# The lo parts of 22 projection weights made by ScalarE and an accumulating transfer

## The chip, the cores and the metric

The kernel runs on one core of one Trainium2 chip. The metric is device time in microseconds (us) of one execution, taken as the median of three runs. The profile is one execution of the same program, recorded by the hardware profiler.

## The reference

One layer of a diffusion backbone: 128 context tokens and 1024 latent tokens, width 1024, in float32. After a modulated RMS norm, one projection gives queries, keys and values of four heads, two halves of a convolution channel, and 16 blocks of gates. Then come differential attention, a depthwise convolution of width 31, their gated merge, an output projection, and a gated MLP. Cut to what matters here:

```python
proj = h @ lp['w_in']                       # q, k, v, u (convolution), g (gates)
a = softmax(s1) - lam * softmax(s2)         # s1, s2: scores of the two halves of q and k
attn_out = rmsnorm(a @ v).reshape(B, T, ATTN_W) @ lp['w_attn_proj']
glu = u[..., :CONV_CH] * sigmoid(u[..., CONV_CH:])
cv = silu(layernorm(dwconv(glu, lp['w_conv_dw'])))       # DW_WIDTH = 31
merged = sigmoid(g[..., :D_MODEL]) * attn_out + sigmoid(g[..., D_MODEL:]) * (cv @ lp['w_conv_proj'])
```

## The kernel before

All large products are made of fp32r matmuls on split operands: x = hi + lo, where hi is x rounded to fp32r and lo the rest. `mm3` (L242) does three matmuls for each block of 128 x 128 weights: hi·hi, hi·lo and lo·hi. A weight unit is a tile of 128 x 1024 (512 KB). SyncE loads it into a `raw` tile (two buffers, L144); ScalarE copies it to `whi` (L180); then `wlo` = raw - whi is made, by a subtraction on GpSimd (L187), or, for most units of the up projection (`by_dma`), by a ScalarE pass that writes minus hi (L183) and a transfer issued on GpSimd that adds raw to it (L184). `whi` and `wlo` have three buffers each. `prep_to` does this for all units up to a position of the sequence SEQ; `take` hands a unit out and notes how far to prepare next: in a projection unit, once its first third is drained, the next two units are prepared.

The attention (`phase1`) runs as four heads of nine query tiles. Each tile has two score products (S, L786 and L787, one tile of three banks), VectorE's minimum (mx, L793), ScalarE's exponential (e, L795), VectorE's weighted difference of the two (e, L806), transposes on TensorE (T, L819) with their split into hi (ath, L822, ScalarE) and lo (atl, L823, VectorE), and the product with the values (O, L834). Between these steps a generator, `fillers`, feeds the matmuls of 22 projection units named in FILL (q1 to q3, k1 to k3, ua2, ub2, ua3, ub3 and gates g0 to g11), paced by a table of numbers. The units q and k go through rope products on GpSimd (L558 to L567). Each `ub` unit starts a depthwise convolution of 31 taps: for each tap VectorE multiplies and adds 967 columns (conv, L651), ScalarE multiplies the other 200 (tap, L658, one buffer) and GpSimd adds them (L664). The split is the constant CSPLIT = 967. The gate units after g11 are named TAIL and are prepared like all others.

Which instruction comes next on an engine is laid out when the program is built: the tile framework simulates a timeline (`schedule_with_timeline_sim=True`) and lists instructions by priority and by the simulated times; attention steps carry a higher priority (HP), and `pin` ties the orders of SyncE, TensorE and VectorE to the written one within a window. On the chip each engine runs its list in order, so a waiting instruction holds up all that follow it on its engine. On GpSimd these are the rope products, the tap sums, the lo subtractions and its transfers.

Of the kernel before, what the change touches and what calls it, by code (L numbers as in the profile page):

```python
# [83 lines left out]
def _w_order():  # L84
    order = ["q0", "k0", "ua0", "ub0", "ua1", "ub1", "v0", "v1", "v2", "v3"]
    fill = FILL_SEQ.split()
    tail = [f"g{i}" for i in range(16) if f"g{i}" not in fill]
    merge = [f"m{j}" for j in range(8)]
    wo = [f"wo{j}" for j in range(8)]
    up = [f"{c}{i}" for i in range(NFF) for c in ("fa", "fb")]  # L90
    down = [f"d0_{h}" for h in range(2)] + [f"e{g}_{u}" for g in range(1, NGRP) for u in range(4)]

    ffn = up[:2] + [f"w{i}_{u}" for i in range(1, NFF) for u in range(4)] + down
    return order, fill, tail, merge, wo, up, down, ffn


ORDER, FILL, TAIL, MERGE, WO, UP, DOWN, FFN = _w_order()
# [12 lines left out]
class Kernel:  # L110
# [80 lines left out]

    def by_dma(self, name):

        if name[0] != "w" or name[1] == "o":
            return False
        i, u = map(int, name[1:].split("_"))
        return i > 1 and u < 3
# [1722 lines left out]
```

## Time and profile before

| | us |
|---|---|
| median of three runs | 1790.59 |
| lowest, highest | 1790.53, 1791.32 |
| the profiled execution | 1790.29 |
| its span, first to last instruction | 1788.3 |
| mean granted TensorE clock | 0.982 |

In the views, PE is TensorE, PEld its weight loads, DVE VectorE, ACT ScalarE, POOL GpSimd and SP SyncE; L187 is line 187 of the kernel. A stretch such as 345:420 is in us from the first instruction. The V products of the attention run up to about 190 us, the heads with their fillers from there to about 705, the merge from there to some 860, then the output projection, the up projection (about 1000 to 1490) and the down projection.

### The profile page before, as it was taken

What the parts mean: (1) busy time and instruction counts of PE and PEld (TensorE: products, weight loads), DVE (VectorE), ACT (ScalarE), POOL (GpSimd) and SP (SyncE); (2) the same over time, 40 slices, a digit from 0 to 9 for tenths busy, and PEclk for the clock granted to TensorE, in tenths of its full rate; (3) what the DMA queues carried; (4) which work ended last, traced back from release to release, by engine and by line L of the source; (5) the groups of instructions that cost most, each with busy time, mean ns of one, the idle gap of its engine ahead of it and who ended that gap; (6) DMA issues with size and microseconds to landing.
All of it is one profiled execution on the core that took longest, in us unless ns stands there. A gap on an engine that the chain in (4) does not pass through costs nothing.

```text
span 1788.3 us, 25510 instructions
## 1 busy us (share of the span) xinstructions
PE 1682.3 (94%) x9928; PEld 1644.2 (92%) x9928; DVE 1177.2 (66%) x1594; ACT 751.1 (42%) x1166; POOL 713.3 (40%) x507
## 2 busy tenths in 40 slices
PE   5999989989989999889989899999999999999997
PEld 3889989978989999888989899999999999999997
DVE  5859995699697663587588765766567565333335
ACT  4424444445454554311225744545455456111111
POOL 2545782585673431544243321222222137433311
PEclk8999999999999999999999999999999999999999
DMA  8264323323325433666753364756666567622102
GB/s 312 88 190 137 103 79 104 132 69 118 120 76 182 142 105 114 235 221 205 268 174 106 85 173 114 182 131 162 150 151 150 139 148 224 175 89 101 62 12 106
DMA packets 111087, 251.96 MB, mean 141 GB/s; under 512 B 10964, under 2 KB 61816, under 8 KB 108920
## 3 DMA queue, kind: packets, MB, share of 16 engines
q1 hardware_dynamic: 45264, 120.15, 19.7%
q10 hardware_dynamic: 51592, 79.08, 13.9%
q0 software_dynamic: 14112, 51.12, 13.4%
q8 instruction: 78, 1.28, 0.3%
q14 instruction: 41, 0.34, 0.1%
HBM read 161.55 MB, written 57.30 MB: 122 GB/s over the span
## 4 chain that ended last, share of the span: by engine, by line
PE 52%; DVE 18%; DMA 8%; issue 8%; POOL 5%; ACT 3%; ACTq 1%; POOLq 0%; DVEq 0%; SPq 0%
PE f L242 15%; PE T L242 7%; DVE conv L651 7%; PE S L1499 6%; PE f L1499 6%; PE T L1499 6%; PE O L242 3%; PE O L1499 3%; DVE mx L793 2%; DMA tg<-scr_gscr 2%; PE O L834 2%; DVE e L806 2%; POOL wlo L187 1%; DVE S L1206 1%; DMA hx<-in_ada 1%
## 5 line engine op out<-in xcount | busy, mean ns | idle before, releaser
L187 POOL TENSOR_TENSOR wlo<-raw,whi 128x1024 fp32r<-128x1024 f32 x104 | 270.2, 2599 | 389.0 <-ACT whi L180 370.8
L242 PE MATMUL f<-h1h,whi 128*128 128x384 f32 x680 | 233.4, 345 | 3.9 <-ACT gt L614 3.2
L242 PE MATMUL f<-h1l,whi 128*128 128x384 f32 x680 | 234.5, 345 | 0.0
L180 ACT CAST whi<-raw 128x1024 fp32r<-128x1024 f32 x126 | 132.0, 1048 | 243.7 <-DMA raw<-in_wst 59.4
L242 PE MATMUL f<-h1h,wlo 128*128 128x384 f32 x680 | 232.0, 342 | 0.0
L1491 DVE SCALAR_TENSOR_TENSOR X<-X,vec,X 128x1153 f32<-128x1153 f32 x88 | 139.7, 1593 | 91.6 <-ACT X L1489 91.0
L651 DVE SCALAR_TENSOR_TENSOR conv<-glu,vec,conv 128x967 f32<-128x967 f32 x120 | 199.2, 1660 | 1.1
L664 POOL TENSOR_TENSOR conv<-conv,tap 128x200 f32<-128x200 f32 x120 | 115.5, 962 | 68.3 <-ACT tap L658 65.8
L242 PEld LDWEIGHTS f<-h1h,whi 128*128 128x128 f32 x680 | 130.2, 192 | 5.3 <-ACT gt L614 3.9
L242 PEld LDWEIGHTS f<-h1l,whi 128*128 128x128 f32 x680 | 130.7, 192 | 0.4
L242 PEld LDWEIGHTS f<-h1h,wlo 128*128 128x128 f32 x680 | 130.2, 192 | 0.2
L795 ACT ACTIVATE e<-S,mx 128x1152 f32<-128x1152 f32 (+1 forms) x72 | 81.2, 1128 | 70.2 <-DVE mx L793 58.7
L793 DVE TENSOR_REDUCE mx<-S 128x1 f32<-128x1152 f32 (+1 forms) x72 | 88.6, 1231 | 31.5 <-PE S L787 31.5
L658 ACT ACTIVATE tap<-glu,vec 128x200 f32<-128x200 f32 x120 | 55.5, 462 | 105.6 <-POOL conv L664 89.9
L242 PE MATMUL T<-ff,whi 128*128 128x384 f32 x360 | 92.1, 335 | 1.5 <-ACT hx L1691 1.5
L184 POOL DMA_DIRECT2D wlo<-rawx x40 | 34.4, 860 | 141.6 <-ACT wlo L183 122.9
L242 PE MATMUL f<-ff,whi 128*128 128x384 f32 x340 | 87.0, 335 | 0.5 <-ACT hx L1691 0.5
L786 PE MATMUL S<-K,q 128*128 128x384 f32 (+1 forms) x200 | 69.0, 345 | 13.3 <-ACT e L795 13.3
L823 DVE TENSOR_TENSOR atl<-T,ath 128x512 fp32r<-128x512 f32 (+1 forms) x100 | 52.0, 538 | 30.3 <-ACT ath L822 29.8
L1251 DVE SCALAR_TENSOR_TENSOR hx<-f,g,hx 128x128 f32<-128x128 f32 (+1 forms) x64 | 31.6, 515 | 58.8 <-PE f L242 58.8
L180 ACT CAST whi<-rawx 128x1024 fp32r<-128x1024 f32 x42 | 44.0, 1047 | 62.0 <-PE S L1499 23.7
L1251 DVE SCALAR_TENSOR_TENSOR hx<-T,g,hx 128x256 f32<-128x256 f32 (+1 forms) x66 | 32.3, 511 | 54.7 <-PE T L242 54.3
(438 smaller groups left out, 4961.6 us busy)
## 6 DMA issues: line engine op xcount, KB each, us to landing
raw<-in_wst SPq DMA_DIRECT2D x105, 512.0 KB, 4.2
wlo<-rawx POOLq DMA_DIRECT2D x40, 512.0 KB, 6.0
X<-scr_fscr POOLq DMA_DIRECT2D x20, 576.0 KB, 5.0
scr_fscr<-X SPq DMA_DIRECT2D x22, 512.0 KB, 5.3
wlo<-raw POOLq DMA_DIRECT2D x20, 512.0 KB, 4.8
scr_gscr<-gate ACTq DMA_DIRECT2D x48, 192.0 KB, 2.0
tg<-scr_gscr SPq DMA_DIRECT2D x24, 384.0 KB, 4.2
ada<-in_ada SPq DMA_DIRECT2D x8, 1024.0 KB, 9.9
```

The costliest lines, as they stand in the source:

```text
L180: nc.scalar.copy(hi, raw)
L187: eng.tensor_tensor(out=lo, in0=raw, in1=hi.bitcast(F32), op=ALU.subtract)
L242: nc.tensor.matmul(out, lhsT=a, rhs=b, start=(i == 0), stop=(i == n - 1))
L651: t = nc.vector.scalar_tensor_tensor(out=o, in0=glu[:, j:j + CSPLIT], scalar=w[:, j:j + 1], in1=o, op0=ALU.mult, op1=ALU.add)
L658: nc.scalar.activation(out=p, in_=glu[:, CSPLIT + j:CONVW + j], func=AF.Copy, scale=w[:, j:j + 1])
L664: t = nc.gpsimd.tensor_tensor(out=o, in0=o, in1=p, op=ALU.add)
L786: nc.tensor.matmul(S[:, j, :cw], lhsT=qt[:, c, o:o + 128], rhs=self.K[:, c, ks], start=True, stop=False)
L793: nc.vector.tensor_reduce(out=mx[:, 1:2], in_=src, axis=AX.XY, op=ALU.min)
L795: nc.scalar.activation(out=e[:, :w].rearrange("p (a b) -> p a b", a=nk), in_=src, func=AF.Exp, scale=-1.0, bias=mx[:, 1:2], accum_out=self ...
L1251: nc.vector.scalar_tensor_tensor(out=d, in0=ps[:, o:o + ln], scalar=gate[:, j, c:c + 1], in1=d, op0=ALU.mult, op1=ALU.add)
L1491: nc.vector.scalar_tensor_tensor(out=y[:, :L], in0=u[:, t:t + L], scalar=w[:, t:t + 1], in1=y[:, :L], op0=ALU.mult, op1=ALU.add)
L1499: nc.tensor.matmul(ps[:, :CH], lhsT=a[:, ws], rhs=b[:, k], start=first and k == 0 and i == 0, stop=last and k == 3 and i == 2)
```

## The change

`by_dma` returns true for every unit in FILL as well. For these 22 units the lo part is then made by a ScalarE pass (L183 in the kernel before) and an accumulating transfer (L184) in place of GpSimd's subtraction (L187). CSPLIT and everything else written in the kernel stay.

```diff
     def by_dma(self, name):
 
+        if name in FILL:
+            return True
         if name[0] != "w" or name[1] == "o":
             return False
         i, u = map(int, name[1:].split("_"))
```

## Rows read from the trace of the kernel before

**Rows 1.** The page, part 1: busy us, share of the span, instructions.

```profile
PE 1682.3 (94%) x9928; PEld 1644.2 (92%) x9928; DVE 1177.2 (66%) x1594; ACT 751.1 (42%) x1166; POOL 713.3 (40%) x507
```

**Rows 2.** Stretches: length, busy PE, PEld, DVE, ACT, POOL; clock, DMA share, GB/s.

```profile
186.00:212.00 26.00, 23.40 (x140) 23.09 (x139) 25.79 (x23) 11.83 (x24) 19.18 (x15) 0.93 0.27 83
212.00:260.00 48.00, 42.41 (x248) 40.24 (x247) 45.90 (x42) 24.58 (x48) 39.00 (x25) 0.96 0.29 79
...
345.00:420.00 75.00, 66.31 (x392) 61.95 (x391) 72.48 (x69) 38.79 (x77) 61.18 (x38) 0.98 0.34 92
...
460.00:560.00 100.00, 90.72 (x546) 86.95 (x545) 90.98 (x91) 49.80 (x100) 71.73 (x47) 0.98 0.32 94
560.00:705.00 145.00, 143.79 (x926) 142.12 (x925) 85.05 (x131) 76.50 (x148) 46.24 (x44) 1.00 0.37 127
```

**Rows 3.** The chain's shares by line, in 186:212, 345:420 and 460:560.

```profile
by line: DVE conv L651 78.5%; issue 11.4%; DVE e L806 6.2%; DVE mx L793 4.9%; DVE e L1018 3.9%; DVE mx L804 0.4%; DVE mx L803 0.3%
...
by line: DVE conv L651 39.1%; DVE e L806 16.3%; DVE mx L793 13.5%; DVE atl L823 7.2%; PE f L242 6.5%; ACT e L795 3.4%; PE T L819 2.9%; DVE mx L804 1.9%; issue 1.9%; DVE sw L550 1.8%; DVE conv L648 1.4%; ACTq L775 0.8%; DVE mx L803 0.8%; PE 
...
by line: DVE conv L651 39.5%; DVE mx L793 14.0%; DVE e L806 9.6%; PE f L242 8.2%; DVE atl L823 7.6%; issue 3.6%; PE O L834 3.1%; POOL conv L664 2.1%; POOL ors L917 1.8%; DVE conv L648 1.7%; DVE sw L550 1.5%; DVE mx L804 1.4%; PE S L786 1.1%
```

**Rows 4.** Groups by line, GpSimd, 160:605: count, busy us, mean ns, idle before.

```profile
L187 POOL TENSOR_TENSOR wlo<-raw,whi 128x1024 fp32r<-128x1024 f32 x23 | 63.0, 2739 | 90.7 <-ACT whi L180 73.5 <-issue 17.0
```

**Rows 5.** The line of the convolution's taps: ns min/median/max, first and last start.

```profile
L651 DVE SCALAR_TENSOR_TENSOR conv<-glu,vec,conv x120: 1208/1385/3457, 123.1 to 564.6; 128x967 f32<-128x967 f32 x120
```

**Rows 6.** Timelines of VectorE and GpSimd, 192:203 and 356:361: start, us, instruction.

```profile
194.48 3.03 DVE L651 SCALAR_TENSOR_TENSOR conv<-glu,vec,conv 128x967 f32<-128x967 f32 x1
...
193.30 3.19 POOL L187 TENSOR_TENSOR wlo<-raw,whi 128x1024 fp32r<-128x1024 f32 x1
...
197.88 3.36 POOL L187 TENSOR_TENSOR wlo<-raw,whi 128x1024 fp32r<-128x1024 f32 x1
...
359.26 2.08 DVE L651 SCALAR_TENSOR_TENSOR conv<-glu,vec,conv 128x967 f32<-128x967 f32 x1
...
357.02 3.30 POOL L187 TENSOR_TENSOR wlo<-raw,whi 128x1024 fp32r<-128x1024 f32 x1
```

**Rows 7.** The chain in order of time, in 140:262: start, us, what.

```profile
199.02 3.25 DVE conv L651
...
235.37 3.29 POOL wlo L187
```

**Rows 8.** The subtraction L187 alone by stretches: length, busy DVE, POOL.

```profile
186.00:212.00 26.00, 0.00 (x0) 6.55 (x2) 0.93 0.27 83
...
345.00:420.00 75.00, 0.00 (x0) 9.04 (x3) 0.98 0.34 92
460.00:560.00 100.00, 0.00 (x0) 10.73 (x4) 0.98 0.32 94
```

**Rows 9.** Lines L183 and L184: ns min/median/max, starts; the transfers' landing.

```profile
L183 ACT ACTIVATE wlo<-whi x60: 1040/1061/1073, 1015.5 to 1466.4; 128x1024 fp32r<-128x1024 f32 x60
...
L184 POOL DMA_DIRECT2D wlo<-rawx x40: 850/859/874, 1023.5 to 1467.7; - x40
...
DMA to landing us min/median/max: 4.5/5.6/10.1
```

**Rows 10.** TensorE's waits in 186:605: us in total, times, longest.

```profile
PE S L786 <- ACT e L795: 13.0, 12, 2.6
```

**Rows 11.** Waits of all engines in 205:705: us in total, times, longest.

```profile
POOL wlo L187 <- ACT whi L180: 97.1, 17, 18.1
...
ACT tap L658 <- POOL conv L664: 57.3, 41, 7.1
```

**Rows 12.** ScalarE's timeline: the hi part of g0, the last drain of q1.

```profile
192.19 1.03 ACT L180 CAST whi<-raw 128x1024 fp32r<-128x1024 f32 x1
...
213.66 0.47 ACT L606 ACTIVATE xs<-f 128x384 f32<-128x384 f32 x1
```

**Rows 13.** DMA queues in 1000:1470: packets, MB, share of 16 engines.

```profile
q0 software_dynamic: 8716, 31.77, 36.5%
```

## The prediction, made before the change was built

> **What bounds the kernel now.** I read the page's busy shares first: TensorE is busy 94% of the span, GpSimd 40%, ScalarE 42% [rows 1]. What GpSimd does matters only where TensorE waits, so I went on by stretches, around the 22 filler units, whose lo parts are made between 168 and 604 us. In the table of stretches [rows 2] read TensorE's and VectorE's busy time against the length. In 186:212, 345:420 and 460:560 VectorE is busy 25.79 + 72.48 + 90.98 = 189 of 201 us, GpSimd 152, and TensorE sits idle 2.6 + 8.7 + 9.3 = 20.6 us; in 212:260 it is idle 5.6 us. In 560:705 it is idle 1.2 of 145 us. So the attention has stretches bound by VectorE (where the convolution's taps run) and stretches bound by TensorE, and an edit here can win at most some 26 us, plus what the granted clock (0.93 to 0.98 there, 1.00 in 560:705) gives back. The chain's shares by line say the same [rows 3]: VectorE's lines make 94% of the chain in 186:212, 82% in 345:420 and 75% in 460:560 (conv, e, mx, atl, sw added up).
>
> **What the change removes.** `by_dma` becomes true for the 22 names in FILL, nothing else. So 22 of the 104 subtractions on GpSimd go. In 160:605 the 23 of them (22 of fillers and v3) take 63.0 us, 2.74 us each [rows 4]. What that is worth on VectorE is read from convolution taps that ran beside one. A tap takes 1.21 us at the least, 1.385 at the median [rows 5]. The one that began at 194.48 beside the subtraction of 193.30 took 3.03; the one at 359.26 beside that of 357.02 took 2.08 [rows 6]; the one at 199.02, beside the subtraction that began at 197.88 and took 3.36, took 3.25 [rows 6, 7]. Against the median these are 1.65, 0.70 and 1.87 us, mean 1.4. The subtractions stretch too, from 2.36 at the least to above 3.
>
> The Trainium skill, "SBUF — State Buffer", section "Who interferes with whom", says that a VectorE instruction with two SBUF inputs contends with a GpSimd instruction that reads SBUF, and that the second to issue is blocked until the first ends. By it a tap could lose a whole subtraction, and the term below would be nearly twice as large; the rows agree that they contend but show both sides losing a part, so the rows' price is used.
>
> The three stretches hold 2 + 3 + 4 = 9 subtractions [rows 8]. 9 x 1.4 = 12.6 us of VectorE time; weighted by the chain's share (94% for 2, 82% for 3, 75% for 4, mean 82%) 10.3 us at most reach the chain. Of that I take half, **5.2 us gained**: GpSimd is 76% busy in these stretches, so its next rope product or tap sum moves into most of the freed time and meets VectorE there; and where VectorE gets ahead, the next thing late is a score bank or a ScalarE copy. Ends: 0 and 10.3.
>
> In 212:260 a subtraction stands on the chain itself, 3.29 us at 235.37 [rows 7], between two rope products. An issue of 0.86 us there would save 2.4. **1.5 gained**, since what follows is waiting for ScalarE soon after; ends 0 and 2.4.
>
> **What it adds.** Each unit gets a second ScalarE pass, minus hi, of 1.06 us [rows 9]: 22 x 1.06 = 23.3 us, 12 of them (12.7 us) in the four stretches where TensorE waits (the 9, and 3 in 212:260). ScalarE is half busy there, for example 38.79 of 75 us [rows 2]. A copy costs time where an exponential stands behind it: TensorE waited for the exponential 13.0 us, 12 times, in 186:605 [rows 10], about 3% of that stretch, and its own row makes 3.4% of the chain in 345:420 [rows 3]. I take a tenth of the 12.7, **1.3 lost**; ends 0 and 12.7.
>
> The accumulating transfer's issue holds GpSimd 0.86 us in place of 2.74. It waits for the lo pass, so GpSimd stands about 1.06 us longer at that place when it comes early; behind it are the convolution's tap sums and the rope products, and ScalarE's taps wait for the tap sums (57.3 us, 41 times, up to 7.1) [rows 11]. Wait and issue together, 1.9 us, are less than the subtraction, so nothing is charged; the end on the bad side is 1.06 us for each of the 9, if every such wait is on the chain, and the good side is a gain of 0.8 each. GpSimd waits for hi already, 97.1 us in 205:705 [rows 11], mostly where it has nothing else.
>
> The lo part lands later: 1.06 + 0.86 + 5.6 us (10.1 at the most) [rows 9] after hi, 7.5 to 12.0 us, instead of 2.4 to 3.4. Cover: the unit g0, one of the two with the least slack, has hi ready at 193.2, and the unit ahead of it drains its last bank at 213.66 [rows 12], 20.4 us later. Later fillers are prepared two units ahead. Nothing is charged. The raw tile is freed some 5 us later, and so SyncE's next raw load starts later; that queue carries only raw loads here, and the same slack covers it. The transfers themselves: 60 of them, with the other accumulating traffic small, took 36.5% of 16 engines over 470 us [rows 13], 2.9 us each; the DMA share of 0.32 to 0.34 in the long stretches [rows 2] would rise to about 0.45. Nothing charged, ends 0 and 2 us.
>
> The Trainium skill, the same page, section "SBUF: two separate sides", speaks against the change: a transfer issued on GpSimd has its descriptors written there, and VectorE instructions in a two-port mode keep it from that. By it some landings would be later still, at VectorE's pleasure. The issue rows agree with no such delay at the issue (850 to 874 ns over 40); where the landing suffers is the third rival below.
>
> The planner lays out every engine's order anew from changed costs, so the places of score, tap and filler work shift by more than the edit. No row prices that; the nearest are a stretch of 48 us in which TensorE idles 5.6 us (212:260) and one of 145 us in which it idles 1.2 (560:705) [rows 2]. About their difference, 4 us, goes to either side in the range, and nothing in the sum. Sum: 5.2 + 1.5 - 1.3 = 5.4 us. The profiled execution took 1790.29 us (its span 1788.3, with 2.0 around it), so 1784.9; the median of the runs is 0.3 above it: **1785 us**.
>
> **The rivals.**
> 1. *The freed time doesn't reach TensorE.* VectorE waits instead for the scores and the exponential, and GpSimd's next work takes the place of the subtraction. For it: GpSimd's 76% in the same stretches, and ScalarE's waits for tap sums. Gains of 0 to 3 us: 1790, from 1787 to 1794. 0.23.
> 2. *Slower: the lo passes get ahead of the exponentials* in the loop score, minimum, exponential, next score, in 212:260, 345:420 and 460:560, where the bank of scores is single. Price 1.06 us a copy; it decides from the seventh of the 12, as 7 x 1.06 eats the 6.7 gained. With all 12: 12.7 - 6.7 = 6 us lost, 1796; without the gain, 1803. For it: 13.0 us of waiting for the exponential; against: ScalarE is half idle there, and its lines make under 5% of the chain in 345:420. 0.17.
> 3. *Late lo parts*: TensorE waits for a landing. It needs one more than 20 us after hi where 12.0 is the most the rows give; each would cost the excess, some us. 1793. 0.02.
> 4. *More than forecast*: the stretches are bound by VectorE and GpSimd together, and the whole 10.3 + 2.4 comes, with 1 to 3 us of the clock that the idle time costs: 1776 to 1780, here 1777. For it: 189 of 201 us busy. 0.12.
> 5. The edit does nothing, because no name matches: FILL is the split list of unit names that `prep_to` passes. 1790. 0.01.
>
> **How the numbers follow.** The forecast, 1781 to 1787, has 0.45. A difference under 0.2% (3.6 us) is about what a measurement of this kernel can't tell from none. Faster by more: 0.45 + 0.12 = 0.57. Within: 0.23 + 0.01 = 0.24. Slower: 0.17 + 0.02 = 0.19. The range goes from rival 4's end to the middle of rival 2's, 1776 to 1797, and leaves out some 0.15.
>
> **What would show it.** Right: GpSimd's subtractions 82, accumulating issues 82, ScalarE's minus-hi passes 82; GpSimd busy some 42 us less over the span, ScalarE 23 more; the mean tap nearer 1.4 than it is, and no 3 us taps beside a weight's preparation; TensorE's idle time between 186 and 605 down by about 5 us, and the merge beginning as much earlier. Wrong: taps shorter but TensorE's idle time unchanged (rival 1); more waiting of score matmuls for the exponential (rival 2); filler matmuls waiting for a transfer (rival 3). I would also be wrong if the gain of the attention were given back in the merge or later, by an order that the planner changed there.

## The result and the profile after

The changed kernel took 1805.65 us in the median (1802.37 to 1810.62, six runs) beside 1791.13 for the kernel before (1790.53 to 1794.21, six runs): ratio 1.0085, interval 1.0073 to 1.0097. It is 15 us slower where 5 us faster had been forecast, and above the end of the range. Single executions of some kernels here went far slower, at a lower granted clock (one of e5 below: 2053.62 us at 0.751), and the ratios leave those out. Lines behind `by_dma` have moved by two: the taps are L653 (L650 the first tap), the rope products L560 and L564, tap sums L666, gates L619, transposes T L821, the split atl L825, the value product O L836.

The edit did what it says. First row: busy us, share and count of each engine, against [rows 1]; then the groups of the three lines that make lo parts (count, busy us, mean ns, idle before).

```profile
PE 1686.6 (94%) x9928; PEld 1648.2 (91%) x9928; DVE 1168.0 (65%) x1594; ACT 771.0 (43%) x1188; POOL 649.3 (36%) x507
...
L187 POOL TENSOR_TENSOR wlo<-raw,whi 128x1024 fp32r<-128x1024 f32 x82 | 209.3, 2554 | 301.0 <-ACT whi L180 297.3
L184 POOL DMA_DIRECT2D wlo<-raw x42 | 36.9, 879 | 219.0 <-ACT wlo L183 125.3
L183 ACT ACTIVATE wlo<-whi 128x1024 fp32r<-128x1024 f32 x82 | 86.6, 1059 | 2.9 <-DMA qz<-scr_qscr 1.5
L184 POOL DMA_DIRECT2D wlo<-rawx x40 | 34.0, 851 | 142.1 <-ACT wlo L183 123.3
```

GpSimd is busy 64 us less, VectorE 9 us less, ScalarE 20 us more, and yet the span grew from 1788.3 to 1803.5. The same stretches as [rows 2]:

```profile
186.00:212.00 26.00, 23.53 (x137) 23.21 (x136) 25.75 (x26) 14.87 (x29) 14.88 (x18) 0.93 0.55 139
212.00:260.00 48.00, 42.47 (x250) 40.82 (x249) 43.47 (x44) 27.65 (x53) 35.10 (x26) 0.96 0.43 108
345.00:420.00 75.00, 63.44 (x361) 60.51 (x361) 70.28 (x65) 35.81 (x70) 43.65 (x33) 0.91 0.39 100
460.00:560.00 100.00, 86.75 (x511) 83.95 (x510) 84.80 (x82) 51.53 (x101) 56.01 (x48) 0.93 0.41 110
560.00:705.00 145.00, 139.78 (x876) 136.69 (x875) 88.67 (x124) 77.47 (x142) 38.49 (x44) 0.99 0.47 145
```

TensorE does less in 345:420 (63.44 for 66.31 us), in 460:560 (86.75 for 90.72) and in 560:705 (139.78 for 143.79), at a lower granted clock. To place the loss I numbered the matmuls (9928 in both traces) and took the start of each after the change minus its start before: -2.2 us at 250, +2.5 at 300, +1.0 at 340, **+9.5 at 355**, 6.5 at 520, **+14.6 at 535**, 13.0 at 595, **+18.4 at 610**, 15.2 at the end. So at 250 us the kernel is 2.2 us ahead, and then it loses at a few places, two of which, at 355 and 535, look alike. The second of these, as a timeline of GpSimd, VectorE and the waiting matmul (start, us, engine, line, instruction, idle before):

```profile
523.86 0.87 POOL L184 DMA_DIRECT2D wlo<-raw  x1 [0.98 <-PE O L836]
524.27 12.47 DVE L653 SCALAR_TENSOR_TENSOR conv<-glu,vec,conv 128x967 f32<-128x967 f32 x1
...
524.47 2.21 POOL L560 TENSOR_TENSOR sw<-sw,cst 128x1024 f32<-128x1024 f32 x1
...
526.35 2.19 POOL L560 TENSOR_TENSOR xs<-xs,cst 128x1024 f32<-128x1024 f32 x1
...
528.21 0.82 POOL L666 TENSOR_TENSOR conv<-conv,tap 128x200 f32<-128x200 f32 x1
...
530.66 2.27 POOL L560 TENSOR_TENSOR xs<-xs,cst 128x1024 f32<-128x1024 f32 x1
532.62 0.80 POOL L666 TENSOR_TENSOR conv<-conv,tap 128x200 f32<-128x200 f32 x1
533.11 2.59 POOL L564 TENSOR_TENSOR xs<-xs,sw 128x1024 f32<-128x1024 f32 x1
...
537.39 0.58 PE L836 MATMUL O<-atl,V 128*128 128x256 f32 x1 [7.92 <-DVE atl L825]
```

One tap took 12.47 us; none in the kernel before took more than 3.46 [rows 5]. It began while GpSimd issued an accumulating transfer and ended 1.04 us after the last of seven GpSimd instructions that follow the issue without a wait. VectorE's queue stood behind it, and TensorE 7.92 us behind that; the granted clock then fell to the lower of its two levels for 13.7 us (stretch: length, busy PE, PEld, DVE, ACT, POOL; clock, DMA share, GB/s):

```profile
533.20:546.90 13.70, 8.94 (x34) 8.25 (x35) 12.21 (x12) 3.06 (x7) 3.05 (x3) 0.50 0.04 13
```

At 346 us the first tap (L650, 715 ns at the least) took 6.86 us, to the end of such a stretch and 0.53 us more; in that stretch, though, a weighted difference had got its turn before (342.66 to 345.09). Look at the starts and lengths of GpSimd's instructions: 526.35 comes 0.33 us before 524.47 + 2.21. Each record overlaps the next by about 0.3 us, where it is 0.03 to 0.06 us between back-to-back instructions of the kernel before. I call GpSimd instructions that follow a transfer's issue without a wait a run.

Not every run keeps VectorE out. At 389.80 the same seven instructions follow an issue without a wait, and here VectorE gets its turn: the tap of 390.97 ends 1.02 us after the first product, and none behind it takes more than 2.86 us.

```profile
389.65 1.39 DVE L808 SCALAR_TENSOR_TENSOR e<-e,mx 128x1152 f32<-128x1152 f32 x1
...
389.80 0.87 POOL L184 DMA_DIRECT2D wlo<-raw  x1 [0.63 <-ACT wlo L183]
...
390.41 2.40 POOL L560 TENSOR_TENSOR sw<-sw,cst 128x1024 f32<-128x1024 f32 x1
...
390.97 2.86 DVE L653 SCALAR_TENSOR_TENSOR conv<-glu,vec,conv 128x967 f32<-128x967 f32 x1
```

TensorE's waits in 186:620 (us in total, times, longest) name the places:

```profile
PE T L821 <- DVE atl L825: 12.6, 8, 5.5
...
PE O L836 <- DVE atl L825: 8.9, 2, 7.9
PE f L244 <- ACT gate L619: 4.3, 2, 3.0
```

The third step, at 600 to 610, is of another kind: a filler waits 3.0 us for a gate's copy out of PSUM, ScalarE for the write-out of the columns before.

### The profile page after: what moved, and what is told of

Read it like the earlier page. It is cut to its first block, busy times and chain, and to the rows that moved or that the text cites. A ratio compares the mean times of both kernels' runs of the same rounds, so it can differ in the third digit from the quotient of the medians.

```text
span 1803.5 us, 25581 instructions
## 1 busy us (share of the span) xinstructions
PE 1686.6 (94%) x9928; PEld 1648.2 (91%) x9928; DVE 1168.0 (65%) x1594; ACT 771.0 (43%) x1188; POOL 649.3 (36%) x507
## 5 line engine op out<-in xcount | busy, mean ns | idle before, releaser
L187 POOL TENSOR_TENSOR wlo<-raw,whi 128x1024 fp32r<-128x1024 f32 x82 | 209.3, 2554 | 301.0 <-ACT whi L180 297.3
L653 DVE SCALAR_TENSOR_TENSOR conv<-glu,vec,conv 128x967 f32<-128x967 f32 x120 | 193.9, 1616 | 1.2
L666 POOL TENSOR_TENSOR conv<-conv,tap 128x200 f32<-128x200 f32 x120 | 102.5, 855 | 110.8 <-ACT tap L660 107.7
L244 PEld LDWEIGHTS f<-h1h,whi 128*128 128x128 f32 x680 | 131.3, 193 | 11.5 <-ACT gate L619 4.9
L184 POOL DMA_DIRECT2D wlo<-raw x42 | 36.9, 879 | 219.0 <-ACT wlo L183 125.3
L183 ACT ACTIVATE wlo<-whi 128x1024 fp32r<-128x1024 f32 x82 | 86.6, 1059 | 2.9 <-DMA qz<-scr_qscr 1.5
L184 POOL DMA_DIRECT2D wlo<-rawx x40 | 34.0, 851 | 142.1 <-ACT wlo L183 123.3
L825 DVE TENSOR_TENSOR atl<-T,ath 128x512 fp32r<-128x512 f32 (+1 forms) x100 | 52.2, 540 | 36.0 <-ACT ath L824 35.6
```

Source lines behind the costliest of these rows:

```text
L183: nc.scalar.activation(out=lo, in_=hi.bitcast(F32), func=AF.Copy, scale=-1.0)
L184: nc.gpsimd.dma_start(out=lo.bitcast(F32), in_=raw, accum_op=ALU.add)
L187: eng.tensor_tensor(out=lo, in0=raw, in1=hi.bitcast(F32), op=ALU.subtract)
L244: nc.tensor.matmul(out, lhsT=a, rhs=b, start=(i == 0), stop=(i == n - 1))
L653: t = nc.vector.scalar_tensor_tensor(out=o, in0=glu[:, j:j + CSPLIT], scalar=w[:, j:j + 1], in1=o, op0=ALU.mult, op1=ALU.add)
L666: t = nc.gpsimd.tensor_tensor(out=o, in0=o, in1=p, op=ALU.add)
```

## The experiments

Each experiment's time is the median of its runs, taken beside runs of the kernel before on the same chip; "ratio" is against those, with its interval. e6, e15, e16 and e18 leave out the right lo parts of the 22 units (hi, minus hi or raw stands in their place) and keep the number of matmuls.

| run | us | ratio | interval | longest VectorE instruction, 200:560 |
|---|---|---|---|---|
| kernel before | 1789.6 to 1792.3 | 1 | | 3.51 |
| changed kernel | 1805.65 | 1.0085 | 1.0073 to 1.0097 | 12.47 |
| e1_sixteen | 1794.12 | 1.0026 | 1.0015 to 1.0036 | 3.49 |
| e2_six | 1815.13 | 1.0141 | 1.0125 to 1.0156 | 12.79 |
| e3_tiny | 1807.03 | 1.0097 | 1.0077 to 1.0117 | 8.04 |
| e4_act | 1799.58 | 1.0047 | 1.0030 to 1.0064 | 3.49 |
| e5_traffic | 1796.28 | 1.0036 | 1.0022 to 1.0051 | 3.52 |
| e6_relief | 1787.91 | 0.9991 | 0.9981 to 1.0001 | 3.63 |
| e15_no_transfer | 1787.33 | 0.9982 | 0.9969 to 0.9994 | 3.25 |
| e16_no_pass | 1779.54 | 0.9941 | 0.9923 to 0.9959 | 3.77 |
| e18_plain | 1796.10 | 1.0030 | 1.0020 to 1.0041 | 4.96 |
| e8_late | 1803.96 | 1.0071 | 1.0058 to 1.0085 | 3.77 |
| e12_break | 1800.10 | 1.0054 | 1.0036 to 1.0071 | 9.98 |
| e17_break2 | 1799.88 | 1.0054 | 1.0041 to 1.0067 | 7.94 |
| e13_break_gate | 1818.41 | 1.0153 | 1.0130 to 1.0177 | 10.46 |
| e20_neg_first | 1807.40 | 1.0098 | 1.0085 to 1.0111 | 8.90 |
| e21_neg_break | 1806.61 | 1.0092 | 1.0079 to 1.0105 | 10.80 |
| e22_five | 1797.41 | 1.0040 | 1.0028 to 1.0051 | 4.21 |
| e23_twelve | 1790.07 | 0.9999 | 0.9990 to 1.0009 | 3.49 |

My theory after the first look: a transfer issued by GpSimd directly ahead of back-to-back work makes that work one run which keeps VectorE out to its end. Rivals: back-to-back work alone does it; the transfer's traffic does it; the loss is in ScalarE's passes; or in the order that the planner laid out anew.

### What keeps VectorE out: a small kernel of its own

It computes nothing of the layer; its outputs are zero. A VectorE multiply-add of 967 columns starts beside 0, 3, 6 or 9 GpSimd multiplications, with or without a transfer issued ahead:

```python
def c_big():  trigger(), dma_big(), run(6), dve_two(), close()   # accumulating, 512 KB
def c_tiny(): trigger(), dma_tiny(), run(6), dve_two(), close()  # plain, 4 KB
def c_gap():  trigger(), dma_big(), run(3), dve_two(); ...wait for ScalarE...; run(3, g3), close()
```

> A small kernel of its own; nothing of the reference is computed, all outputs are zero. Nine cases, three times each: a VectorE instruction over 967 columns starts about 1 us into a run of GpSimd multiplications of 128x1024 with no waits between them. Theory (an issue on GpSimd just ahead of a run makes its instructions follow each other without a gap, and VectorE's is kept out to the end of the run): alone 1.1 to 1.2 us; 6 multiplications without a transfer ahead, 2 to 3.5 us; with an accumulating transfer of 512 KB ahead, 4 to 5 us for a run of 3, 10 to 12 for 6, 16 to 18 for 9; with a transfer of 4 KB ahead of 6, again 10 to 12; with a wait put into the middle of the 6, 4 to 5; the same with a one-input VectorE instruction. Rival A (back-to-back work on GpSimd is enough): 6 without a transfer takes as long as 6 with one. Rival B (the traffic does it): 512 KB long, 4 KB as short as without.

Timelines: six multiplications without a transfer, with the accumulating one, with the small one.

```profile
25.58 5.56 POOL L40 TENSOR_TENSOR P<-P,g 128x1024 f32<-128x1024 f32 x2 [25.13 <-ACT g L29]
26.48 2.46 DVE L43 SCALAR_TENSOR_TENSOR D<-g,w,E 128x967 f32<-128x967 f32 x1 [3.43 <-ACT g L30]
...
109.82 0.88 POOL L33 DMA_DIRECT2D acc<-g  x1 [3.94 <-ACT g L29]
110.42 14.09 POOL L40 TENSOR_TENSOR P<-P,g 128x1024 f32<-128x1024 f32 x6
110.50 15.04 DVE L43 SCALAR_TENSOR_TENSOR D<-g,w,E 128x967 f32<-128x967 f32 x1 [3.60 <-ACT g L30]
...
242.31 0.59 POOL L36 DMA_DIRECT2D tiny<-g  x1 [3.94 <-ACT g L29]
242.92 13.81 POOL L40 TENSOR_TENSOR P<-P,g 128x1024 f32<-128x1024 f32 x6
242.99 14.77 DVE L43 SCALAR_TENSOR_TENSOR D<-g,w,E 128x967 f32<-128x967 f32 x1 [3.59 <-ACT g L30]
```

Alone the multiply-add takes 1.10 to 1.23 us. Beside six multiplications without a transfer it waits for the first one's end (27.92), takes its 1.02 us and is done at 28.94; the second multiplication waits for it in turn (3.26 us for 2.34). With a transfer ahead it took 8.2 behind 3 multiplications, 15.04 behind 6, 21.92 behind 9: to the end of the run plus 1.03. A wait of GpSimd in the middle of six cut it to 8.2. The 4 KB plain transfer does nearly the same (14.74 to 14.77), so it is not the traffic, and six without a transfer don't, so it is not the work alone. One thing differs besides: behind a transfer the multiply-add starts some 0.1 us into the first multiplication, without one 0.84 to 0.90 us into it. The kernel before answers that: weighted differences that began 0.06 and 0.05 us into a rope product with more work right behind it (398.59 and 525.20) ended 1.22 us after that product, so an early start alone doesn't do it. The form with one input, the first tap's, took 14.55 with the transfer and 2.02 without. In this kernel the theory holds; its price was larger than I had expected.

### Sixteen transfers, or the six alone

Six issues stand directly ahead of a rope unit's products, because a unit's buffer comes free just when the q or k unit ends whose rope work follows: g1, ub2, g3, ub3, g5 and g7.

```diff
-        if name in FILL:
+        if name in FILL and name not in ("g1", "ub2", "g3", "ub3", "g5", "g7"):   # e1_sixteen
+        if name in ("g1", "ub2", "g3", "ub3", "g5", "g7"):                        # e2_six
```

> The change for 16 of the 22 units; the six whose transfer GpSimd issues just ahead of a unit's rope products (g1, ub2, g3, ub3, g5, g7) keep the subtraction. Theory of the lock-out: no VectorE instruction above 4 us between 186 and 720 us, GpSimd's overlapping runs gone, and the two steps of 8.5 and 9.7 us gone: 1785 to 1794. Rival (ScalarE's 22 extra passes and the transfers' traffic): 16/22 of the 14.5 us lost remains, 1799 to 1803.

> The change for those six units alone. Theory of the lock-out: VectorE instructions of 5 us and more beside the rope products, as in the changed kernel, and most of its loss: 1797 to 1808. Rival (passes and traffic): 6/22 of 14.5 us, 1793 to 1797, with no such instruction.

Without the six, no VectorE instruction above 3.49 us is left in 200:560 and some 11 us come back (11.5 by the medians, 10.6 by the ratios). The six alone, on the kernel before, cost 1.41%, some 25 us, more than I expected; VectorE stands 6.58, 6.85, 9.07 and 12.79 us in its trace. The two costs don't add up (25 + 5 against 15 together): each layout meets other work.

### A 4 KB transfer ahead of the rope products of the kernel before

```diff
+            if h:
+                nc.vector.tensor_copy(self.tiny[:, 0:8], box["sw"][:, 0:8])
+                nc.gpsimd.dma_start(out=self.tiny[:, 8:16], in_=self.tiny[:, 0:8])
```

> The kernel before, and in each of the six rope units a transfer of 4 KB issued on GpSimd between the shuffle and the products (with a VectorE copy of 8 columns that it reads). No extra ScalarE pass, no traffic, all subtractions stay. Theory of the lock-out: some VectorE instructions of 4 us and more in the rope runs, and a loss of 4 to 15 us, 1795 to 1806. Rival: 1790 to 1793, as six issues of under 1 us on GpSimd cost next to nothing.

Six transfers of 4 KB, with all subtractions kept and no pass, cost 1807.03: 0.97%, as much as the whole change. VectorE stood 8.04, 5.43, 5.17 and 3.64 us, at three of the six issues; at the other three nothing took more than 3.53. An issue in this place can cost, whatever it moves.

### The terms of the sum, one by one

```diff
+   e4:  nc.scalar.activation(out=lo, in_=hi.bitcast(F32), func=AF.Copy, scale=-1.0)  # then GpSimd's subtraction
+   e5:  nc.sync.dma_start(out=self.A["tscr"][FILL.index(SEQ[self.prepped])], in_=raw)
+   e6:  lo = hi                                          # no subtraction, no pass, no transfer
-   e15: nc.gpsimd.dma_start(out=lo.bitcast(F32), in_=raw, accum_op=ALU.add)          # the pass stays
+   e16: nc.gpsimd.dma_start(out=lo.bitcast(F32), in_=raw)   # plain copy, no pass
+   e18: nc.gpsimd.dma_start(out=lo.bitcast(F32), in_=raw)   # plain copy, behind the pass
```

> The kernel before, with the 22 filler units' lo parts left out: their hi tile is used in their place, so that GpSimd's 22 subtractions go and nothing comes for them (the products with the lo parts of these weights are then wrong in value, the number of matmuls is the same). It measures the prediction's term for what the removed subtractions are worth: 6.7 us, between 0 and 12.7. If the term is right: 1781 to 1786. If the freed time does not reach TensorE (rival 1): 1789 to 1791.

> The changed kernel with the 22 accumulating transfers left out: the lo tile of a filler unit stays at minus hi (so the products with these lo parts are wrong in value, their number is the same). Subtractions removed and ScalarE's passes added, no issue, no traffic, no wait of GpSimd for the pass. Beside the kernel without the 22 subtractions (1787.9) it gives the price of the passes alone: 1788 to 1790 if they cost the 1.3 us of the prediction, 1794 to 1798 if the kernel with the extra passes (1799.6) showed their own price and not that of the subtraction's second wait.

> The kernel before, with the minus-hi pass of ScalarE added for the 22 filler units; GpSimd's subtraction then overwrites what the pass wrote, so the pass is extra work alone. It adds 22 passes of about 1.06 us to ScalarE and makes each subtraction wait for one more ScalarE instruction. If ScalarE's passes cost what the prediction charged (1.3 us): 1790 to 1793. If rival 2 of the prediction had been right about them (12.7 us at the full price): about 1803.

> The kernel before, with a plain transfer of each filler's raw tile (512 KB, 22 of them, 11.5 MB in all) from SBUF to DRAM added on SyncE's queue: the traffic of the change alone, with no issue on GpSimd. If the traffic is what costs around 586 to 606 us (the landing of the gate's weights and of V): 4 to 8 us there, 1793 to 1798. If it costs the 0 to 2 us of the prediction: 1790 to 1792.

> The changed kernel with the 22 minus-hi passes left out and the transfer made a plain copy of raw (so the lo parts are wrong in value, the number of matmuls is the same). Subtractions removed, issues and traffic and the runs behind the issues as in the changed kernel, no pass. If the loss is in the transfers: 1800 to 1807. If the passes carry it: 1789 to 1796.

> The changed kernel with ScalarE's passes and the transfer's wait for them, but the transfer a plain copy of raw, as in the kernel without passes (so the lo parts are wrong in value, the number of matmuls is the same). If the place of the issue, which the wait for the pass sets, brings the lock-out: long VectorE instructions come back at some of the rope runs, and 1794 to 1806 us. If the accumulation brings the loss: 1778 to 1786.

*Relief.* Without the 22 subtractions the kernel gains 1.6 us (0.9991), not 6.7. Yet VectorE's taps did get shorter. In 186:605 (count, busy us, mean ns), first the kernel before, then e6:

```profile
L651 DVE SCALAR_TENSOR_TENSOR conv<-glu,vec,conv 128x967 f32<-128x967 f32 x90 | 153.7, 1708 | 0.5
```

```profile
L654 DVE SCALAR_TENSOR_TENSOR conv<-glu,vec,conv 128x967 f32<-128x967 f32 x90 | 141.1, 1568 | 0.6
```

That is 12.6 us less, but with 21 subtractions gone; that it equals the sum's 9 x 1.4 is luck. In the three stretches of that sum the mean tap went from 1.64 us (65 taps) to 1.53 (69), some 8 us in all. VectorE stayed as busy there (189 and 188 of 201 us), and TensorE's busy time rose by 1.6 us (180.4 to 182.0). So the time saved on VectorE was put too high, and the share of it that reaches the end as well.

*Passes.* With 22 passes besides (e15), 1787.33: nothing lost. The extra pass in the kernel before (e4) cost 0.47%, but there the subtraction also waits for it. The two together suggest that a pass costs by what waits for it on GpSimd, not by ScalarE's time.

*Traffic.* 22 plain transfers of 512 KB on SyncE's queue cost 0.36% (0.22 to 0.51), some 6 us where the prediction had 0 to 2. Its profile loses them near 200, 235 and 405 us and not near 600 where I had expected them.

*Transfers without the pass.* e16 is 10.6 us faster than before, 26 us faster than the changed kernel, with the same 22 issues and the same bytes. It lies below both ranges that I had set. Its trace around the issue that brought 12.47 us above:

```profile
504.85 0.57 POOL L184 DMA_DIRECT2D wlo<-raw  x1 [1.70 <-PE f L247]
...
506.51 1.36 DVE L555 STREAM_SHUFFLE sw<-xs 128x1024 f32<-128x1024 f32 x1
...
507.96 1.90 POOL L563 TENSOR_TENSOR sw<-sw,cst 128x1024 f32<-128x1024 f32 x1 [2.54 <-DVE sw L555]
508.32 2.56 DVE L656 SCALAR_TENSOR_TENSOR conv<-glu,vec,conv 128x967 f32<-128x967 f32 x1
```

The transfer needn't wait for the copy to hi and the pass, so it goes 1.7 us ahead of VectorE's shuffle; GpSimd then has to wait 2.54 us for the shuffle, and the run is broken before it begins. In the changed kernel the shuffle ran from 522.42 to 523.78 and the transfer was issued at 523.86, right behind it: no wait was left. The pass, which ran from 522.49 to 523.57, put the issue there. With the pass back and the copy still plain (e18), the issue stands behind the shuffle again (515.07 to 516.41, issue at 516.43), VectorE instructions of 4.96, 4.63 and 4.11 us come back, and some 16 us are lost again. They end behind the second, fifth and sixth instruction of their runs and are too short to be all of it. Most of the loss thus goes with the wait for the pass, and with accumulation it is larger (1796 against 1806); how much of either step is the new layout was not tested. The place right behind the shuffle isn't enough either: the issue at 389.80 in the changed kernel came 0.05 us behind its shuffle.

### Ways out of the run

```diff
   e8:  # prepare a third later, and queue the issue behind the rope unit's last product
+                with self.tc.issue_after(self.rope_last) if self.rope_last else nullcontext():
   e12: # behind the issue of each of the six: GpSimd, ScalarE, GpSimd, one column
+                    nc.gpsimd.memset(self.brk[:, 0:1], 0.0)
+                    nc.scalar.copy(self.brk[:, 1:2], self.brk[:, 0:1])
+                    t = nc.gpsimd.tensor_copy(self.brk[:, 2:3], self.brk[:, 1:2]).ins
   e17: # e12, and the rope unit's first two products ordered behind t (in e12 the first alone)
   e13: # e12, and the gate's tile from a tag with two buffers
   e20: # minus hi straight from raw, ahead of the copy to hi
   e21: # e17 and e20
```

> The changed kernel, but a weight unit whose preparation falls at the end of a q or k unit is prepared one third later, and its transfer is issued behind that unit's last rope product on GpSimd. So no transfer stands directly ahead of a run of rope products; all 22 lo parts are still made by transfer. If the lock-out of VectorE by the run behind an issue is the cause of the loss: no VectorE instruction of the attention above 4 us, and 1787 to 1796 us. If the loss is in the transfers' traffic, in ScalarE's passes or in the planner's order, it stays near the changed kernel's 1806: 1801 to 1810.

No long instruction is left, but 1803.96. A new wait took a part of its place: near 504 us the matmuls fall 6 us behind, and more is lost near 385 and 600. The late transfers run beside the rope units' write-outs. The write-out's landing (KB each, median us) in 186:640, and TensorE's wait behind it in 480:640:

```profile
scr_qscr<-xs ACTq DMA_DIRECT2D x6, 288.0 KB, 6.7
```

```profile
PE f L247 <- ACT xs L613: 3.4, 1, 3.4
```

In the kernel before this write-out took 3.0 us, and that wait was not there.

> The changed kernel, with a round trip behind the transfer's issue of g1, ub2, g3, ub3, g5 and g7: GpSimd writes one column, ScalarE copies it, GpSimd copies it back, and the first rope product comes behind that. All 22 transfers stay, at the same places and times; only GpSimd has to wait once between the issue and the run of rope products. If it is the unbroken run behind an issue that keeps VectorE out: no VectorE instruction of the attention above 4 us, and about what the changed kernel with 16 transfers gave, 1792 to 1798 us. If the transfers' landing beside the rope products is the cause, or the traffic, or the passes: 1802 to 1808, with the long taps still there.

> The kernel with the round trip, now with the first two rope products of a unit behind it (in the kernel before it, in two of the six units the second product had gone ahead of the round trip, and a tap of 7.94 and one of 9.98 us stood there). If the unbroken run behind the issue is the cause: no VectorE instruction of the attention above 4 us, and 12 us less than the kernel with the round trip gave, 1786 to 1792 us. If accumulation, traffic or the wait for the pass carry the loss: 1798 to 1803.

> The kernel with the round trip, and the gate's tile in a tag with two buffers, so that ScalarE need not wait for the write-out of the gate's columns before. If the write-outs that land later beside the transfers are what is left of the loss around 600 us (4 to 5 us): 2 to 5 us below the kernel with the round trip, 1788 to 1795. If they cost nothing there: the same as it.

> The changed kernel with ScalarE's two passes in the other order: minus hi is made straight from raw, and the copy to hi comes behind it, so that the transfer can be issued about 1.06 us earlier, all work kept. If the place of the issue against the shuffle that frees the rope run decides: fewer long VectorE instructions, and 1784 to 1798 us. If not: 1803 to 1808.

> The last kernel with the round trip of e17 as well. If the two causes are one (the run without a wait): the same as e17, 1786 to 1792. If the earlier issue brings something of its own (the lo part lands earlier, GpSimd stands less): up to 8 us below e17, 1778 to 1786.

e12 and e17 give some 6 us back, not the 8 to 20 expected. Where GpSimd did wait in the round trip the taps behind it are no longer than the kernel before has them (2.48 and 2.69 us in e17; up to 3.46 before). But between the issue and the copy the planner had put other ready work, so at three or more of the six issues in e12 and at two in e17 no wait of GpSimd stands behind the issue. At two of these in e12 VectorE stood, 7.94 and 9.98 us, and at one in e17, 7.94; at the others (383.43 in e12, 385.26 in e17) it got its turn as at 389.80. e21 shows that the extra instructions without a wait don't end it:

```profile
384.36 0.87 POOL L189 DMA_DIRECT2D wlo<-raw  x1 [2.55 <-ACT wlo L185]
...
384.94 0.40 POOL L192 MEMSET brk<- 128x1 f32 x1
385.00 1.64 POOL L681 TENSOR_TENSOR conv<-conv,tap 128x200 f32<-128x200 f32 x1
...
386.60 1.12 POOL L194 COPY brk<-brk 128x1 f32<-128x1 f32 x1
...
387.68 1.90 POOL L574 TENSOR_TENSOR sw<-sw,cst 128x1024 f32<-128x1024 f32 x1
388.87 10.80 DVE L668 SCALAR_TENSOR_TENSOR conv<-glu,vec,conv 128x967 f32<-128x967 f32 x1
```

None of these GpSimd rows has a wait noted behind the issue, and the tap stands 10.80 us. Here the records overlap by 0.03 us, as little as behind the small plain transfer (0.03 to 0.06), so an overlap of 0.3 us is not needed for it. Every VectorE instruction above 4 us in 150:610 of these traces stands where GpSimd hasn't waited since an issue, but not every such place has one. e20, with the issue meant to come one pass earlier, still has runs of 8.90, 8.51 and 8.10 us. e13 was a miss: the gates' tag is shared with other tiles, and the kernel became 18 us slower than e12; which of its waits made that I did not settle. Nor does the one long tap explain all of e21's 1806.6.

### What is left without long instructions

```diff
+        if name in ("g0", "k1", "ua2", "ua3", "g6"):                                # e22_five
+        if name in FILL and name not in ("g1", "ub2", "g3", "ub3", "g5", "g7", "g8", "g9", "g10", "g11"):  # e23_twelve
```

> The kernel with 16 transfers, less the four that are issued from 545 us on (g8 to g11), where TensorE is the bound and the relief buys nothing. If the loss of 5 us around 600 came from these transfers beside the load of V and the gates' write-outs: 3 to 5 us below the kernel with 16, 1788 to 1791 us. If it came from elsewhere: 1793 to 1796.

> The changed kernel with the transfer for g0, k1, ua2, ua3 and g6 alone, the five whose subtraction stood in a stretch where VectorE is the bound and whose issue is not directly ahead of rope products; the other 17 keep the subtraction. If the removed subtractions are worth what the kernel without all 22 showed (2 us) and five transfers cost little: 1786 to 1791 us, with no VectorE instruction of the attention above 4 us. If every transfer costs: 1791 to 1795.

e23 is e1 without the four transfers of the stretch bound by TensorE, and 4 us faster. In the 25 us around the change of heads near 590 V lands after 9.1 us in e1 and 5.9 in e23, and ScalarE waits for the gates' write-outs (us in total, times, longest), first e1, then e23:

```profile
ACT gate L619 <- DMA scr_gscr<-gate: 14.5, 4, 5.2
```

```profile
ACT gate L619 <- DMA scr_gscr<-gate: 8.9, 3, 5.9
```

e1 lost 4 us there and e23 nothing; in the kernel before V landed in 5.6 us. The third step of the changed kernel is at the same change of heads (V 9.3 us there). That V's landing is the cause isn't shown: e23 has four passes and four issues less besides, and in e6 and e15, without any of these transfers, V takes 7.3 and 7.4 us at this change. e22 was a miss, 1797.41 for 1786 to 1791: a transfer (234.77) came directly ahead of a rope subtraction, with a tap of 4.21 us, and the rest of its loss I cannot name. No version that computes the layer beats the kernel before; e23 equals it.

## Why the prediction was wrong, point by point

**What bounds it, and what the edit removes.** Right: the counts and ScalarE's busy time (20 us more for 23). GpSimd's busy time fell by 64 us where 42 had been forecast. Two of the three large steps stand in stretches where TensorE waits, as the prediction had it; the third, near 600, stands in 560:705, where it had charged nothing.

**The price of an overlap was too high and wrong in kind.** It came from the three longest taps that began inside one of the nine subtractions. Two more did, and inside four of the nine none began; the five together took 5.5 us over the median, which is 0.6 for each of the nine where the sum has 1.4. And the prediction read "both sides losing a part". The rows say something stricter: of the taps in 160:605 of the kernel before, 78 began while a GpSimd instruction of over 0.5 us was running, and they end 1.02 us after that instruction's end (5th to 75th percentile; 95th 1.07). The rows at hand had it already [rows 6]: 193.30 + 3.19 + 1.02 = 197.51, and the tap ends at 194.48 + 3.03 = 197.51; 357.02 + 3.30 + 1.02 = 361.34, and 359.26 + 2.08 = 361.34. The Trainium skill, "SBUF — State Buffer", section "Who interferes with whom", states this: whoever issues first holds the shared pair for the whole instruction and the other blocks. These rows agree with it; I had set the rule aside on a reading of durations where I should have read ends. Who gets the turn when that instruction ends, the prediction never asked: in the kernel before it was VectorE, behind some issues GpSimd time after time. The traces show a pattern that no run was made to test. In 150:610 of the changed kernel and the experiments, 40 issues are followed by three or more GpSimd instructions of over 0.5 us without a wait. At 14 of them a VectorE instruction with two inputs in SBUF was already running when the issue began (as 389.65 above), and no VectorE instruction behind these took over 4 us; at the other 26 none was, and 20 of these have one that did. The kernels share much of their layout, so these are not 40 independent cases.

**The share that reaches the end: the term was mis-sized.** Half of 10.3, and 1.5: e6 measured 1.6 in all (-0.2 to 3.4). Rival 1 was right on this term, "the freed time doesn't reach TensorE".

**The passes.** 1.3 lost: e15 against e6 shows nothing. Rival 2's mechanism, passes ahead of exponentials, isn't in the profile: score matmuls waited for the exponential 11.5 us in 186:605, 13.0 before.

**The step that failed** is "Wait and issue together, 1.9 us, are less than the subtraction, so nothing is charged". It counted how long GpSimd is held and not what the issue does to what comes next, though the prediction itself named the rope products as queued behind it. Measured: some 11 us for the six on top of the other sixteen, 25 alone, 17 for 4 KB transfers in their places; in the changed kernel two of the six, at 339.14 and 523.86, kept VectorE out. The wait for the pass, 1.06 us a unit on the prediction's bad side, seems to have done its harm by place: it set issues right behind the shuffle (e16 against e18). "The issue rows agree with no such delay" was true and beside the point: the sufferer is not the issue but VectorE.

The trace of the kernel before had a small case that hints at it, outside the stretches that I read. Near 1500 us GpSimd issues transfers back to back and then subtracts. VectorE's second X (1500.93, 4.70 of the 7.09 us of the two) begins before the subtraction and yet ends 1.23 us after it; that is one instruction, not a run:

```profile
1498.54 7.09 DVE L1491 SCALAR_TENSOR_TENSOR X<-X,vec,X 128x1153 f32<-128x1153 f32 x2 [4.37 <-ACT X L1489]
1499.59 1.83 POOL L1695 DMA_DIRECT2D hx<-scr_xscr  x2
1500.75 1.24 POOL L1653 DMA_DIRECT2D X<-scr_fscr  x1
1501.31 3.09 POOL L187 TENSOR_TENSOR wlo<-raw,whi 128x1024 fp32r<-128x1024 f32 x1
```

Of the 60 issues of the up projection, 40 of which gave the costs of [rows 9], 59 have no GpSimd instruction behind them without a wait, so their rows could not show it.

**Traffic: mis-sized.** 0 to 2 us; e5 measured 6, and four transfers less (e23 against e1) gave 4. The mean share of the DMA engines says little. Where the time goes stays open: e5 lost nothing near 600, where e1 lost its 4.

**Late lo parts** (rival 3): no filler's matmul waited for a transfer.

**The order.** 4 us to either side was too little. e6, e15 and e16 remove the same subtractions and end at 1787.9, 1787.3 and 1779.5: those that do more end no later than the one that does least, so something besides these terms, most likely the new layout, moves the time by up to 8 us. Why e16 is 8 us faster than e6 stays open, and with it how much of the changed kernel's 26 us over e16 is the runs alone. An accumulating transfer that doesn't wait for the pass was not tried.

## What to carry to other kernels

Price a transfer issued by GpSimd by what GpSimd does next: if back-to-back work follows without a wait, and VectorE has instructions with operands in SBUF to do, put the whole length of that work on VectorE as the bad end. Take a saving on an engine that is busy 94% as an upper end, and ask who is late next before counting half of it. Judge contention by the ends of the two instructions, and take costs for a moved operation from rows with the same work behind it.

## What the runs showed of the hardware

- A VectorE multiply-add of 967 columns that starts inside a GpSimd instruction ends 1.02 us after it (78 taps); GpSimd's next one is stretched in turn (3.26 for 2.34 us).
- Behind a transfer's issue, GpSimd instructions that follow without a wait can keep VectorE out to the last of them: in the small kernel 8.2, 15.04 and 21.92 us for 3, 6 and 9 multiplications of 2.3 us; a 4 KB transfer is enough (14.77), and a wait of GpSimd ends it (8.2). In the layer, with three or more GpSimd instructions behind, 20 of 40 such issues have a VectorE instruction above 4 us, and none of the 14 does at which a VectorE instruction with two SBUF inputs was running when the issue began.
- The accumulating issue takes 0.87 us and the next instruction starts 0.26 us before it ends; the plain issue takes 0.57 us and the next starts behind it.
- In most runs that kept VectorE out behind an accumulating issue the records of GpSimd's instructions overlap by some 0.3 us (at 523.86); in e21's at 384.36 by 0.03.
